# Both value projections first, the two kinds of heads in turn, the output projection in passes of six and two heads, and a square on ScalarE in the norm's Newton step

## The chip, the cores and the metric

The kernel runs on one core of one Trainium2 chip. The metric is the device time of one execution in microseconds (us). In three runs the kernel before took 1231.18, 1232.57 and 1232.76 us; the median is 1232.57 us. The engines are named as the profile names them: PE is TensorE, with PEld for its weight loads, DVE is VectorE, ACT is ScalarE, POOL is GpSimd, and SP is the queue that issues the DMAs.

## The reference

Two layers work on 512 tokens of width 1024. Each layer normalises x, projects it into seven parts of 512 columns, runs four retention heads and four stick-breaking heads of width 128, normalises each head, projects the eight heads back and adds them to x. A gated feed-forward block of width 2816 follows.

```python
h = rms_norm(x, norm1_g[l])
proj = h @ w_in[l]
rq, rk, rv, rg, sq, sk, sv = jnp.split(proj, IN_SPLITS, axis=-1)
ret = chunk_retention(apply_rotary(to_heads(rq, N_RET_HEADS)),
                      apply_rotary(to_heads(rk, N_RET_HEADS)),
                      to_heads(rv, N_RET_HEADS))
ret = from_heads(head_group_norm(ret, ret_norm_g[l])) * jax.nn.silu(rg)
sb = stick_breaking(to_heads(sq, N_SB_HEADS), to_heads(sk, N_SB_HEADS), to_heads(sv, N_SB_HEADS))
sb = from_heads(head_rms_norm(sb, sb_norm_g[l]))
x = x + jnp.concatenate([ret, sb], axis=-1) @ w_out[l]
h = rms_norm(x, norm2_g[l])
x = x + (jax.nn.silu(h @ w_gate[l]) * (h @ w_up[l])) @ w_down[l]
```

## The kernel before

Activations are held transposed: 8 tiles `x[k]` of 128 features by 512 tokens. Every fp32 matrix product is made of three fp32r matmuls on a high and a low part of both operands (`mm3`, line 184); the parts are written by ACT (`hi`) and by DVE or POOL (`lo`). Weights come as 1024-column units, each loaded by one DMA on SP and split into `whi` (ACT, line 127) and `wlo` (DVE, line 128); three units are held at a time.

The order on PE is written out by the program. The projections run one after another, and each small step of a head is put down with `pe.later(delay, fn)`, to be issued between two groups of three matmuls once the program's own count of PE time has gone by. The other engines take their work in an order that a scheduler fixes when the program is built, each strictly in turn.

In a layer the values of the stick-breaking heads come first (`SV`), then for each of four heads its `SQ`, `SK` and the gate columns `RG`, then the values of the retention heads (`RV`), then `RQ` and `RK` of four heads. A stick-breaking head makes scores (`z`), takes absolute value, exponential and logarithm on ACT (lines 513 to 515), an operation `e` and a scan on DVE (lines 516 and 523), transposes on PE (`turn`), and a product with the values (`weighted`, into bank `o`). A retention head rotates q and k (DVE lines 426 to 428, the sum on POOL in line 430), makes scores, multiplies by a decay (`p`) and makes the same product. Both end in `normed`: ACT squares the product (`sq`, line 476), the square's parts `shi` and `slo` are multiplied by ones into bank `o` (these are called the sums below), and `rsqrt` makes the inverse root from them: Ln and Exp on ACT (lines 309 and 310), then one Newton step in three DVE operations (lines 311, 314, 317), and a fourth multiplies the head by it (line 487). The head's parts `mhi` and `mlo` go into the output projection.

PSUM has three banks `acc`, four banks `z`, and a single bank `o`, which takes the product and the sums of every head in turn. The output projection takes the four stick-breaking heads for all eight tiles of x first, then the retention heads for tiles 0 to 3 and for tiles 4 to 7, in both with the last head set apart. When a tile of x is complete, `feed` makes its parts `hhi` (ACT) and `hlo` (DVE) for the feed-forward block and adds its square into `ssq` (ACT and POOL). The feed-forward block needs the sum over `ssq` (`token_scale`, parts `sshi` and `sslo`, into bank `o`) after its fourth group of weights.

Of the kernel before, what the change touches and what calls it, by code (L numbers as in the profile page):

```python
# [10 lines left out]
F32 = mybir.dt.float32  # L11
F32R = mybir.dt.float32r
# [29 lines left out]
D_RQK, D_RAV, D_SS = 9000, 9000, 5500  # L42


V_SLOT, QK_SLOT, PT_SLOT, M_SLOT = 0, 8, 12, 18


def block_plan():
# [5 lines left out]

    for l in range(L):
        plan += [("w_in", l, k, SV, 512) for k in range(KT)]
        for h in range(NH):
            for c in (SQ, SK, RG):
                plan += cols("w_in", l, c + h * HD)
        plan += [("w_in", l, k, RV, 512) for k in range(KT)]  # L60
        for h in range(NH):
            plan += cols("w_in", l, RQ + h * HD) + cols("w_in", l, RK + h * HD)
        for d in range(KT):
            plan += [("w_out", l, NH + k, d * P, P) for k in range(NH)]
        for d0 in range(0, KT, 4):
            ds = range(d0, d0 + 4)
            plan += [("w_out", l, k, d * P, P) for d in ds for k in range(NH - 1)]
            plan += [("w_out", l, NH - 1, d * P, P) for d in ds]
# [76 lines left out]
class Stream:  # L145
# [20 lines left out]
    def run(self, i):  # L166
        self.inside = True
        self.tasks.pop(i)[1]()
        self.inside = False

    def drain(self):
        while self.tasks:
            self.run(min(range(len(self.tasks)), key=lambda n: self.tasks[n][0]))

    @staticmethod
    def cost(n):
# [25 lines left out]
def layers(ctx, tc, xT_in, ws_in, gcol_in, gfin_in, cos_in, sin_in, dec_in, out):  # L202
# [137 lines left out]
    def attention(l):  # L340
        g0 = l * NG
        with tc.tile_pool(name=f"at{l}", bufs=1, reuse_waits="tile") as sb:
# [25 lines left out]
            def proj_v(col, evac):  # L368

                pss = banks_a() if col == SV else [bank() for _ in range(3)] + [bank("z", 4)]  # L370
                v = [
                    [slot(V_SLOT + TB * i + tb, n) for tb in range(TB)]
                    for i, n in enumerate(("vhi", "vlo"))
                ]

                def step(tb, k, w):
                    c = slice(tb * P, tb * P + P)
# [95 lines left out]
            def normed(o, m, key):  # L473
# [7 lines left out]
                def finish():  # L481
                    ss = bank("o", 1)
                    pe.mm(ss, ones_r, shi, True, False)
                    pe.mm(ss, ones_r, slo, False, True)
                    rn = temp("rn")
                    rsqrt(rn, ss, HD)
                    nc.vector.tensor_tensor(out=m, in0=m, in1=rn, op=ALU.mult)
                    if key < NH:
                        hi, lo = (slot(M_SLOT + 2 * key + i, n) for i, n in enumerate(("mhi", "mlo")))
                    else:  # L490
                        hi = sb.tile([P, S], F32R, tag="mhi", name="mhi", bufs=4)
                        lo = sb.tile([P, S], F32R, tag="mlo", name="mlo", bufs=4)
                    split(hi, lo, m)
                    mix[key] = hi, lo
# [95 lines left out]
            for h in range(NH):  # L590
                ps = proj(SQ + h * HD)
                q = sb.tile([P, S], F32, tag="q", name="q", bufs=1)
                nc.vector.scalar_tensor_tensor(
                    out=q, in0=ps, scalar=float(HD) ** -0.5, in1=rs, op0=ALU.mult, op1=ALU.mult
                )
                q = parts(q, "q")
                ps = proj(SK + h * HD)
                k = sb.tile([P, S], F32, tag="k", name="k", bufs=1)
                nc.vector.tensor_tensor(out=k, in0=ps, in1=rs, op=ALU.mult)
                k = parts(k, "k")  # L600
                pe.later(D_SQK, lambda h=h, q=q, k=k, v=v: stick(h, q, k, v))
                ps = proj(RG + h * HD)
                nc.vector.tensor_tensor(out=gate[:, h], in0=ps, in1=rs, op=ALU.mult)
# [8 lines left out]
            for h in range(NH):  # L612
                q = rotated(proj(RQ + h * HD), "q")
                k = rotated(proj(RK + h * HD), "k")
                pe.later(D_RQK, lambda h=h, q=q, k=k, v=v: retain(h, q, k, v))
# [5 lines left out]
            for d in range(KT):  # L621
                ps = bank()
                for k in range(NH):
                    out_step(ps, d, NH + k, k == 0, k == NH - 1)
                nc.vector.tensor_tensor(out=x[d], in0=x[d], in1=ps, op=ALU.add)
            for d0 in range(0, KT, 4):
                pss = dict(zip(range(d0, d0 + 4), banks_b() if d0 else banks_a()))
                for d, ps in pss.items():
                    for k in range(NH - 1):
                        out_step(ps, d, k, k == 0, False)  # L630
                pe.drain()
                for d, ps in pss.items():
                    out_step(ps, d, NH - 1, False, True)
                    nc.vector.tensor_tensor(out=x[d], in0=x[d], in1=ps, op=ALU.add)
                    feed(d, g0 + 8)

    def ffn(l):
        last = l == L - 1
# [176 lines left out]
```

## Time and profile before

| what | value |
|---|---|
| three runs | 1231.18, 1232.57, 1232.76 us |
| the profiled execution, its own time | 1231.52 us |
| its span, first to last instruction | 1229.7 us |
| mean granted clock of PE over the span | 0.996 |
| busy PE, PEld, DVE, ACT, POOL | 1211.7, 999.1, 693.4, 489.4, 164.9 us |
| DMA traffic over the span | 93 GB/s |

The busy time of an engine is a share of the whole span; what an engine costs the end is read from the waits and the chain. A matmul's recorded duration overlaps the next one's, so the distance from start to start, not the duration, is its price. The granted clock is given as a share: 1.00 is 2.4 GHz, 0.50 is 1.2 GHz.

### The profile page before, as it was taken

Reading aid. Unit: us, or ns where it says so; the run is one execution under the profiler, and the core shown is the slowest. Engines: PE = TensorE matmul, PEld = TensorE weight load, DVE = VectorE, ACT = ScalarE, POOL = GpSimd, SP = SyncE. Lnnn points to the kernel's source line nnn. Section 1 sums busy time; section 2 is a strip of 40 time slices with the busy share of each in tenths; the row PEclk is TensorE's granted clock in tenths of the full one; section 3 lists DMA queues with packets and bytes.
Section 4 is the critical chain, followed back from the end, with each engine's and each line's share of the span. In section 5 each row is a group of like instructions: output and inputs, shape, how many; then the busy total and the mean of one; then the engine's idle time right before and its main releaser. Section 6 shows DMA issues by size and latency. Waiting matters only on the chain.

```text
span 1229.7 us, 13902 instructions
## 1 busy us (share of the span) xinstructions
PE 1211.7 (99%) x5474; PEld 999.1 (81%) x5474; DVE 693.4 (56%) x861; ACT 489.4 (40%) x708; POOL 164.9 (13%) x142
## 2 busy tenths in 40 slices
PE   8999999999999999999999999999999999999997
PEld 6888887888888888888888888878888888888886
DVE  5557799785443344444444778997644433444433
ACT  5456643453232122233344766445433212223323
POOL 3221044030000000000112212432100000000021
PEclk9999999999999999999999999999999999999999
DMA  6221221222222322324222222212222223322221
GB/s 240 86 72 66 85 98 59 87 91 98 102 86 103 103 86 103 102 87 138 97 92 87 69 69 86 86 69 103 101 82 93 103 71 105 116 96 93 103 86 69
DMA packets 33329, 115.74 MB, mean 94 GB/s; under 512 B 3824, under 2 KB 3824, under 8 KB 33264
## 3 DMA queue, kind: packets, MB, share of 16 engines
q1 hardware_dynamic: 33120, 114.83, 27.1%
q8 instruction: 43, 0.70, 0.2%
q14 instruction: 22, 0.18, 0.0%
q10 hardware_dynamic: 144, 0.02, 0.0%
HBM read 112.75 MB, written 2.10 MB: 93 GB/s over the span
## 4 chain that ended last, share of the span: by engine, by line
PE 93%; DVE 4%; issue 2%; POOL 1%; DMA 1%; ACT 1%; SPq 0%; DVEq 0%; ACTq 0%; POOLq 0%
PE acc L181 71%; PE z L181 16%; PE o L181 4%; PE z L192 1%; DMA wraw<-ws 1%; DVE ptlo L285 1%; DVE wlo L128 1%; DVE hlo L288 0%; DVE u L311 0%; DVE mlo L285 0%; POOL slo L285 0%; DVE m L580 0%; DVE t L428 0%; DVE t L426 0%; DVE p L571 0%
## 5 line engine op out<-in xcount | busy, mean ns | idle before, releaser
L127 ACT CAST whi<-wraw 128x1024 fp32r<-128x1024 f32 (+1 forms) x205 | 214.7, 1048 | 492.2 <-PE acc L181 223.7
L181 PE MATMUL acc<-hhi,whi 128*128 128x512 f32 x960 | 376.0, 392 | 0.0
L181 PE MATMUL acc<-hhi,wlo 128*128 128x512 f32 x960 | 373.9, 389 | 0.0
L181 PE MATMUL acc<-hlo,whi 128*128 128x512 f32 x960 | 373.7, 389 | 0.0
L128 DVE TENSOR_TENSOR wlo<-wraw,whi 128x1024 fp32r<-128x1024 f32 (+1 forms) x205 | 258.0, 1259 | 131.5 <-ACT whi L127 130.7
L181 PEld LDWEIGHTS acc<-hhi,wlo 128*128 128x128 f32 x960 | 180.2, 188 | 37.9
L181 PEld LDWEIGHTS acc<-hhi,whi 128*128 128x128 f32 x960 | 180.3, 188 | 36.3
L181 PEld LDWEIGHTS acc<-hlo,whi 128*128 128x128 f32 x960 | 180.3, 188 | 36.2
L684 DVE TENSOR_TENSOR u<-acc,rs 128x512 f32<-128x512 f32 x40 | 27.7, 691 | 134.5 <-PE acc L181 134.5
L301 POOL TENSOR_TENSOR ssq<-ssq,sqx 128x512 f32<-128x512 f32 x28 | 44.7, 1598 | 392.1 <-ACT sqx L300 391.4
L681 DVE TENSOR_TENSOR g<-acc,rs 128x512 f32<-128x512 f32 x40 | 27.7, 692 | 89.9 <-PE acc L181 89.9
L181 PE MATMUL acc<-ahi,whi 128*128 128x512 f32 x176 | 68.5, 389 | 0.0
L181 PE MATMUL acc<-alo,whi 128*128 128x512 f32 x176 | 68.5, 389 | 0.0
L181 PE MATMUL acc<-ahi,wlo 128*128 128x512 f32 x176 | 68.5, 389 | 0.0
L748 POOL TENSOR_TENSOR xtd<-xtd,gfin 128x512 f32<-128x512 f32 x7 | 10.2, 1453 | 345.7 <-ACT fsq L744 345.7
L288 DVE SCALAR_TENSOR_TENSOR hlo<-x,gcol,hhi 128x512 fp32r<-128x512 f32 x32 | 38.7, 1227 | 9.0 <-ACT hhi L287 9.0
L181 PEld LDWEIGHTS acc<-alo,whi 128*128 128x128 f32 x176 | 33.0, 188 | 6.9
L181 PEld LDWEIGHTS acc<-ahi,whi 128*128 128x128 f32 x176 | 33.0, 188 | 6.8
L181 PEld LDWEIGHTS acc<-ahi,wlo 128*128 128x128 f32 x176 | 33.0, 188 | 6.8
L284 ACT CAST ahi<-u 128x512 fp32r<-128x512 f32 x44 | 27.4, 622 | 28.1 <-DVE u L685 28.1
L181 PE MATMUL z<-wlo,hhi 128*128 128x512 f32 x80 | 32.8, 410 | 2.4 <-DVE wlo L128 2.4
L181 PE MATMUL acc<-mhi,whi 128*128 128x512 f32 x88 | 35.1, 399 | 0.0
(189 smaller groups left out, 1818.1 us busy)
## 6 DMA issues: line engine op xcount, KB each, us to landing
wraw<-ws SPq DMA_DIRECT2D x203, 512.0 KB, 3.5
x<-xT SPq DMA_DIRECT2D x8, 256.0 KB, 7.1
dec<-dec SPq DMA_DIRECT2D x8, 256.0 KB, 3.7
out<-ob SPq DMA_DIRECT2D x4, 512.0 KB, 2.6
wraw<-ws SPq DMA_DIRECT2D x2, 256.0 KB, 4.1
cosrs<-cos SPq DMA_DIRECT2D x2, 256.0 KB, 5.8
sinrs<-sin SPq DMA_DIRECT2D x2, 256.0 KB, 5.4
gfin<-gfin SPq DMA_DIRECT2D x1, 512.0 KB, 4.4
```

Source lines behind the costliest of these rows:

```text
L127: nc.scalar.copy(out=hi[:, c], in_=raw[:, c])
L128: nc.vector.tensor_tensor(out=lo[:, c], in0=raw[:, c], in1=hi[:, c].bitcast(F32), op=ALU.subtract)
L181: self.nc.tensor.matmul(ps, lhsT=lhsT, rhs=rhs, start=start, stop=stop)
L192: self.nc.tensor.transpose(out, src, ident)
L284: nc.scalar.copy(out=hi, in_=src)
L285: eng.tensor_tensor(out=lo, in0=src, in1=hi.bitcast(F32), op=ALU.subtract)
L288: eng.scalar_tensor_tensor(out=lo, in0=src, scalar=scale, in1=hi.bitcast(F32), op0=ALU.mult, op1=ALU.subtract,)
L301: nc.gpsimd.tensor_tensor(out=ssq, in0=ssq, in1=q, op=ALU.add)
L681: nc.vector.tensor_tensor(out=g, in0=pg, in1=rs, op=ALU.mult)
L684: nc.vector.tensor_tensor(out=u, in0=pu, in1=rs, op=ALU.mult)
L748: nc.gpsimd.tensor_tensor(out=y, in0=y, in1=gfin[:, c], op=ALU.mult)
```

## The change

It concerns the attention part of both layers. The retention values are projected directly behind the stick-breaking values and kept in tiles of their own, since the stick-breaking values are still in use. The heads follow in the order S0 G0 S1 G1 G2 G3 R0 S2 R1 S3 R2 R3, where S is a stick-breaking head, G the gate columns of one head and R a retention head. The gate's Silu follows directly on G3. The output projection takes six heads first (the stick-breaking ones and retention heads 0 and 1): tiles 0 to 2 with four of the heads and then with the other two, tiles 3 to 7 with all six; then heads 2 and 3 for all tiles, with `feed` behind each. In the norm the square of the root is made by ACT, and three DVE operations follow instead of four. The number of matmuls and of weight units is the same.

```diff
+HEADS = [(c[0], int(c[1])) for c in "S0 G0 S1 G1 G2 G3 R0 S2 R1 S3 R2 R3".split()]
+STICKS = tuple(range(NH, 2 * NH))
+FIRST, NEXT = STICKS[:-1] + (0,), (STICKS[-1], 1)
...
+                    return sb.tile([P, S], F32R, tag=f"{n}{tb}", name=n, bufs=1)
...
-                    rn = temp("rn")
-                    rsqrt(rn, ss, HD)
-                    nc.vector.tensor_tensor(out=m, in0=m, in1=rn, op=ALU.mult)
+                    r, t = temp("rn"), temp("sq")
+                    act(out=r, in_=ss, func=AF.Ln, scale=1.0 / HD, bias=eps)
+                    act(out=r, in_=r, func=AF.Exp, scale=-0.5)
+                    act(out=t, in_=r, func=AF.Square, scale=0.125)
+                    nc.vector.scalar_tensor_tensor(
+                        out=t, in0=ss, scalar=HD * EPS, in1=t, op0=ALU.add, op1=ALU.mult
+                    )
+                    nc.vector.scalar_tensor_tensor(
+                        out=t, in0=t, scalar=6.0, in1=r, op0=ALU.subtract, op1=ALU.mult
+                    )
+                    nc.vector.scalar_tensor_tensor(
+                        out=m, in0=m, scalar=-0.25, in1=t, op0=ALU.mult, op1=ALU.mult
+                    )
...
-            v = proj_v(SV, evac_sv)
+            sv = proj_v(SV, evac_sv)
+            rv = proj_v(RV, evac_rv)
...
-            v = proj_v(RV, evac_rv)
-            pe.later(10000, silu_gate)
...
+                    if h == NH - 1:
+                        silu_gate()
...
+                while k not in mix:
+                    pe.advance()
...
+            half = FIRST + NEXT
+            pss = [bank() for _ in range(3)]
+            for d, ps in enumerate(pss):
+                for k in FIRST:
+                    out_step(ps, d, k, k == half[0], False)
+            for d, ps in enumerate(pss):
+                for k in NEXT:
+                    out_step(ps, d, k, False, k == half[-1])
+                add(d, ps)
+            for d in range(3, KT):
+                ps = bank()
+                for k in half:
+                    out_step(ps, d, k, k == half[0], k == half[-1])
+                add(d, ps)
+            pss = banks_a()
+            for d, ps in enumerate(pss):
+                out_step(ps, d, 2, True, False)
+            pe.drain()
+            for d, ps in enumerate(pss):
+                out_step(ps, d, 3, False, True)
+                add(d, ps)
+                feed(d, g0 + 8)
+            for d in range(4, KT):
+                ps = bank()
+                out_step(ps, d, 2, True, False)
+                out_step(ps, d, 3, False, True)
+                add(d, ps)
+                feed(d, g0 + 8)
```

`pe.advance()` issues the waiting step that is due first; `add` is the sum into `x[d]` on DVE.

In what follows, the PE work that lies between two instructions is counted from the order, at 0.227 us for 512 columns (1488 matmuls in 337.28 us) and in proportion for fewer.

**Place 1: a head's product in bank `o`, and what PE does next.** A name with its number is one tile. On PE before, in layer 0, the end of one retention head's product (o_1804), followed by projection (acc) and the next head's scores (z):

```order
L181 MATMUL o_1804<-ptlo_1707,vhi_1153 128x256
L181 MATMUL o_1804<-pthi_1706,vlo_1157 128x256
L181 MATMUL acc_1791<-hhi2_129,whi27_1637 128x512
L181 MATMUL acc_1791<-hlo2_137,whi27_1637 128x512
L181 MATMUL acc_1791<-hhi2_129,wlo27_1638 128x512
L181 MATMUL z_1830<-qhi_1632,khi_1729 128x512
L181 MATMUL z_1830<-qlo_1633,khi_1729 128x512
```

The next use of bank `o` before, the sums o_1877, comes behind 5.7 us of matmuls. On PE of the changed kernel, the end of the product of retention head 1 (o_1606), the sums of stick-breaking head 2 (o_1627), and projection:

```order
L186 MATMUL o_1606<-pthi_1498,vhi_387 128x256
L186 MATMUL o_1606<-ptlo_1499,vhi_387 128x256
L186 MATMUL o_1606<-pthi_1498,vlo_391 128x256
L186 MATMUL o_1627<-shi_1550,ones_r_118 128x512
L186 MATMUL o_1627<-slo_1551,ones_r_118 128x512
L186 MATMUL acc_1520<-hhi5_132,whi24_1373 128x512
```

The next use of the single bank has moved directly behind the product, with no matmul between. The operations that read o_1606 stand on DVE behind operation `e` and the scan of the next stick-breaking head (scores z_1563), then DVE's product m_1619, then ACT's square sq_1621; that square is what o_1627 waits for. From the end of z_1563 to o_1627 PE has 2.9 us of matmuls.

**Place 2: the sums of a head, and how bank `o` comes free.** On PE before, 27 matmuls (6.1 us) stand between the sums o_1877 and the next product o_1948. On ACT before, at the same sums (r_1881 is Ln, then Exp):

```order
L127 CAST whi30_1905<-wraw30_1796 128x1024
L309 ACTIVATE r_1881<-o_1877,eps_120 128x512
L310 ACTIVATE r_1881<-r_1881 128x512
L127 CAST whi31_1939<-wraw31_1909 128x1024
L284 CAST mhi_1889<-m_1817 128x512
L284 CAST khi_1900<-k_1898 128x512
L476 ACTIVATE sq_1963<-o_1948 128x512
```

On DVE lines 311 and 314 follow, the last read of the sums. On PE of the changed kernel, at the sums of stick-breaking head 3 (o_1913) and the product of retention head 2 (o_1931):

```order
L186 MATMUL o_1913<-shi_1862,ones_r_118 128x512
L186 MATMUL o_1913<-slo_1863,ones_r_118 128x512
L186 MATMUL acc_1884<-mhi_1393,whi28_1720 128x512
L186 MATMUL acc_1884<-mlo_1394,whi28_1720 128x512
L186 MATMUL acc_1884<-mhi_1393,wlo28_1721 128x512
L186 MATMUL o_1931<-pthi_1825,vhi_385 128x512
```

And on ACT there, where rn_1916 is Ln and then Exp, and sq_1917 the square that has come to ACT:

```order
L129 CAST whi30_1886<-wraw30_1791 128x1024
L289 CAST shi_1862<-sq_1860 128x512
L289 CAST khi_1879<-k_1877 128x512
L233 ACTIVATE rn_1916<-o_1913,eps_120 128x512
L129 CAST whi31_1952<-wraw31_1890 128x1024
L233 ACTIVATE rn_1916<-rn_1916 128x512
L233 ACTIVATE sq_1917<-rn_1916 128x512
L289 CAST mhi_1924<-m_1858 128x512
```

Three matmuls are left between the sums and the next product. On ACT the cast khi_1879 has moved ahead of Ln, a weight cast (whi31) between Ln and Exp, and the square behind Exp; DVE's first operation on sq_1917, the last read of o_1913, follows behind wlo31.

**Place 3: the completed tiles of x, at the end of the output projection.** On DVE before (x is the sum, hlo the low part that `feed` makes, wlo a weight unit):

```order
L634 TENSOR_TENSOR x0_86<-x0_86,z_2132 128x512
L634 TENSOR_TENSOR x1_87<-x1_87,z_2133 128x512
L634 TENSOR_TENSOR x2_88<-x2_88,z_2134 128x512
L288 SCALAR_TENSOR_TENSOR hlo0_135<-x0_86,gcol_81,hhi0_127 128x512
L634 TENSOR_TENSOR x3_89<-x3_89,z_2135 128x512
L288 SCALAR_TENSOR_TENSOR hlo1_136<-x1_87,gcol_81,hhi1_128 128x512
L128 TENSOR_TENSOR wlo36_2239<-wraw36_2186,whi36_2238 128x1024
L288 SCALAR_TENSOR_TENSOR hlo2_137<-x2_88,gcol_81,hhi2_129 128x512
L288 SCALAR_TENSOR_TENSOR hlo3_138<-x3_89,gcol_81,hhi3_130 128x512
L128 TENSOR_TENSOR wlo37_2269<-wraw37_2242,whi37_2268 128x1024
L634 TENSOR_TENSOR x4_90<-x4_90,acc_2234 128x512
L634 TENSOR_TENSOR x5_91<-x5_91,acc_2235 128x512
```

On DVE of the changed kernel, from the first completed tile on:

```order
L646 TENSOR_TENSOR x0_86<-x0_86,z_2200 128x512
L646 TENSOR_TENSOR x1_87<-x1_87,z_2201 128x512
L646 TENSOR_TENSOR x2_88<-x2_88,z_2202 128x512
L293 SCALAR_TENSOR_TENSOR hlo0_135<-x0_86,gcol_81,hhi0_127 128x512
L646 TENSOR_TENSOR x3_89<-x3_89,z_2203 128x512
L293 SCALAR_TENSOR_TENSOR hlo1_136<-x1_87,gcol_81,hhi1_128 128x512
L646 TENSOR_TENSOR x4_90<-x4_90,acc_2256 128x512
L130 TENSOR_TENSOR wlo37_2258<-wraw37_2208,whi37_2257 128x1024
L646 TENSOR_TENSOR x5_91<-x5_91,acc_2275 128x512
L293 SCALAR_TENSOR_TENSOR hlo2_137<-x2_88,gcol_81,hhi2_129 128x512
L646 TENSOR_TENSOR x6_92<-x6_92,acc_2288 128x512
L293 SCALAR_TENSOR_TENSOR hlo3_138<-x3_89,gcol_81,hhi3_130 128x512
```

The sums of tiles 4 to 7 have moved in among the low parts of tiles 0 to 3. On PE of the changed kernel 18.4 us of matmuls lie between the end of tile 0 (z_2200) and the sums of `token_scale` (o_2386); before, 23.8 us lie there.

One more move bears on a step below. In the changed kernel the last two operations of the rotation of k of retention head 2 (t2_1709) stand on DVE behind the low part of the second transposed piece of stick-breaking head 3 (z_1753) and behind another head's m_1619. From z_1753 to that retention head's scores z_1810, which need k, PE has 4.9 us of matmuls.

## Rows read from the trace of the kernel before

**Rows 1.** Page, part 1: busy us, share of the span, instructions.

```profile
PE 1211.7 (99%) x5474; PEld 999.1 (81%) x5474; DVE 693.4 (56%) x861; ACT 489.4 (40%) x708; POOL 164.9 (13%) x142
```

**Rows 2.** Chain that ended last, layer 0: start, us, what.

```profile
30.75 5.59 PE z L181 x24
...
278.39 337.28 PE acc L181 x1488
```

**Rows 3.** Waits of PE, whole span: who waited for whom: us, times, longest.

```profile
PE o L181 <- ACT shi L284: 2.6, 2, 1.3
PE z L181 <- DVE wlo L128: 2.4, 1, 2.4
PE o L181 <- POOL slo L285: 2.1, 2, 1.1
...
PE o L181 <- DVE u L314: 0.8, 2, 0.4
PE z L181 <- POOL klo L285: 0.5, 1, 0.5
```

**Rows 4.** Stretches: length, busy time (instructions) by engine, PEclk, DMA share, GB/s.

```profile
24.30:27.60 3.30, 3.30 (x9) 2.60 (x8) 1.12 (x1) 0.00 (x0) 0.00 (x0) 0.50 0.67 231
...
192.00:204.00 12.00, 9.21 (x45) 7.14 (x44) 11.63 (x16) 5.21 (x10) 5.01 (x4) 1.00 0.21 77
204.00:216.00 12.00, 11.53 (x53) 9.24 (x53) 11.91 (x15) 4.00 (x6) 4.74 (x3) 1.00 0.19 56
806.00:809.40 3.40, 3.12 (x8) 2.48 (x9) 3.40 (x4) 2.29 (x4) 1.92 (x2) 0.51 0.02 5
```

**Rows 5.** Timeline, layer 0: start, us, engine, line, operation, [idle before, releaser].

```profile
194.74 0.28 PE L181 MATMUL o<-pthi,vlo 128*128 128x256 f32 x1
...
199.69 0.74 DVE L580 SCALAR_TENSOR_TENSOR m<-o,gcol,gate 128x512 f32<-128x512 f32 x1
...
200.52 0.60 ACT L476 ACTIVATE sq<-o 128x512 f32<-128x512 f32 x1 [5.07 <-DVE m L580]
```

**Rows 6.** DVE by line and shape, 30 to 278 us: busy us, mean ns, idle.

```profile
L311 DVE SCALAR_TENSOR_TENSOR u<-r 128x512 f32<-128x512 f32 x10 | 8.4, 836 | 8.7 <-ACT r L228 6.0 <-ACT r L310 2.7
...
L314 DVE SCALAR_TENSOR_TENSOR u<-o,u 128x512 f32<-128x512 f32 x10 | 6.9, 688 | 0.2
...
L523 DVE TENSOR_TENSOR_SCAN e<-z,e 128x511 f32<-128x511 f32 x4 | 4.9, 1218 | 0.1
```

**Rows 7.** ACT by line and shape, same stretch.

```profile
L127 ACT CAST whi<-wraw 128x1024 fp32r<-128x1024 f32 x37 | 38.9, 1050 | 36.7 <-PE acc L181 20.7 <-PE z L181 8.2 <-issue 7.8
...
L309 ACT ACTIVATE r<-o,eps 128x512 f32<-128x512 f32 x8 | 5.5, 687 | 4.9 <-PE o L181 4.8
...
L310 ACT ACTIVATE r<-r 128x512 f32<-128x512 f32 x8 | 5.1, 632 | 0.2
...
L513 ACT ACTIVATE e<-z 128x512 f32<-128x512 f32 x8 | 4.6, 588 | 4.1 <-PE z L181 4.1
```

**Rows 8.** Timeline of DVE behind the first value projection, layer 0.

```profile
34.37 2.07 DVE L288 SCALAR_TENSOR_TENSOR vlo<-z,rst,vhi 128x512 fp32r<-128x512 f32 x3 [0.76 <-ACT vhi L287]
```

**Rows 9.** Page, part 6: DMA of the decay tables, KB each, us to landing.

```profile
dec<-dec SPq DMA_DIRECT2D x8, 256.0 KB, 3.7
```

**Rows 10.** POOL by line and shape, 30 to 278 us: busy us, mean ns, idle.

```profile
L301 POOL TENSOR_TENSOR ssq<-ssq,sqx 128x512 f32<-128x512 f32 x7 | 11.8, 1683 | 18.8 <-ACT sqx L300 18.6
...
L430 POOL TENSOR_TENSOR k<-t,t 128x512 f32<-128x512 f32 x4 | 7.9, 1985 | 9.3 <-DVE t L428 9.3
```

**Rows 11.** Timeline of DVE, end of the output projection of layer 0.

```profile
243.23 2.05 DVE L634 TENSOR_TENSOR x<-x,z 128x512 f32<-128x512 f32 x3 [0.82 <-PE z L181]
...
249.31 3.48 DVE L288 SCALAR_TENSOR_TENSOR hlo<-x,gcol,hhi 128x512 fp32r<-128x512 f32 x2
...
254.12 2.05 DVE L634 TENSOR_TENSOR x<-x,acc 128x512 f32<-128x512 f32 x3 [0.19 <-PE acc L181]
...
265.24 0.68 DVE L285 TENSOR_TENSOR sslo<-ssq,sshi 128x512 fp32r<-128x512 f32 x1
```

More of the change, by code (lines that the diff above doesn't have):

```diff
@@ L56, in block_plan @@
         plan += [("w_in", l, k, SV, 512) for k in range(KT)]
-        for h in range(NH):
-            for c in (SQ, SK, RG):
+        plan += [("w_in", l, k, RV, 512) for k in range(KT)]
+        for kind, h in HEADS:
+            for c in {"S": (SQ, SK), "G": (RG,), "R": (RQ, RK)}[kind]:
                 plan += cols("w_in", l, c + h * HD)
[L60 to L68, printed above, removed]
+        for ds, ks in OUT:
+            plan += [("w_out", l, k, d * P, P) for d in ds for k in ks]
         for k in range(KT):
@@ L169, in run, with advance @@
         self.inside = False
+    def advance(self):
+        self.run(min(range(len(self.tasks)), key=lambda n: self.tasks[n][0]))
     def drain(self):
         while self.tasks:
-            self.run(min(range(len(self.tasks)), key=lambda n: self.tasks[n][0]))
+            self.advance()
     @staticmethod
@@ L608, in silu_gate @@
                 table_set(EXP_LN)
-            v = proj_v(RV, evac_rv)
-            pe.later(10000, silu_gate)
[L612 to L615, printed above, removed]
+            for kind, h in HEADS:
+                if kind == "S":
+                    ps = proj(SQ + h * HD)
+                    q = sb.tile([P, S], F32, tag="q", name="q", bufs=1)
+                    nc.vector.scalar_tensor_tensor(
+                        out=q, in0=ps, scalar=float(HD) ** -0.5, in1=rs,
+                        op0=ALU.mult, op1=ALU.mult,
+                    )
+                    q = parts(q, "q")
+                    ps = proj(SK + h * HD)
+                    k = sb.tile([P, S], F32, tag="k", name="k", bufs=1)
+                    nc.vector.tensor_tensor(out=k, in0=ps, in1=rs, op=ALU.mult)
+                    k = parts(k, "k")
+                    pe.later(D_SQK, lambda h=h, q=q, k=k: stick(h, q, k, sv))
+                elif kind == "G":
+                    ps = proj(RG + h * HD)
+                    nc.vector.tensor_tensor(out=gate[:, h], in0=ps, in1=rs, op=ALU.mult)
+                    if h == NH - 1:
+                        silu_gate()
+                else:
+                    q = rotated(proj(RQ + h * HD), "q")
+                    k = rotated(proj(RK + h * HD), "k")
+                    pe.later(D_RQK, lambda h=h, q=q, k=k: retain(h, q, k, rv))
@@ L617, in out_step, with add @@
             def out_step(ps, d, k, first, last):
                 w = wst.block("w_out", l, k, d * P, P)
+                while k not in mix:
+                    pe.advance()
                 pe.mm3(ps, w, mix[k], first, last)
-            for d in range(KT):
-                ps = bank()
[L623 to L635, printed above, removed]
+            def add(d, ps):
+                nc.vector.tensor_tensor(out=x[d], in0=x[d], in1=ps, op=ALU.add)
```

24 lines of the change are left out of this document (6 added, 18 removed).

## The prediction

> **What bounds the kernel now.** I read the page's busy times first: PE is busy for 1211.7 us, 99% of the span [rows 1]. In the feed-forward part the chain of work is PE alone, 1488 matmuls in one piece of 337.28 us, 0.227 each [rows 2], and the change keeps the number of matmuls, so it can only move the time in which PE stands still or is slowed. The waits of PE come next [rows 3]: 2.6 + 2.1 + 0.8 + 0.5 = 6.0 us lie in the attention of both layers, half in each, and 2.4 us at the start, which the change doesn't touch. The table of stretches [rows 4] says why: from 192 to 216 us, where the retention heads come one upon another, DVE is busy for 23.5 of 24 us and PE stops. The timeline shows how that reaches PE [rows 5]: a head's product ended at about 195.0, DVE came to read it at 199.69, and ACT squared it at 200.52, right after DVE's reading (0.09 us behind its end); the sums wait for that square.
>
> The clock belongs to this. Behind the stop in layer 1 the granted clock is 0.51 for 3.4 us, the 1.2 GHz level [rows 4]. At half speed PE loses 1.7 us there, less the 0.3 us in which it stood still anyway (busy 3.12 of 3.40): I price such a fall at 1.4 us. The 2.4 us wait at the start was followed by one too, the equal stop in layer 0 by none. So of three stops of 2.3 to 2.4 us, two cost a fall. What the change can win is therefore 6.0 + 1.4 = 7.4 us, 0.6%.
>
> **The norm's Newton step.** Sixteen heads lose one DVE operation with two operands from SBUF (0.84 us mean [rows 6]), 13.4 us in all, and give ACT one square, priced like its Exp at 0.63 us [rows 7], 10.1 us in all. Both run beside PE; ACT is busy for some 40% of the span [rows 1], so I cost the work itself at nothing. It costs where PE waits for the end of that chain, which is in the steps below.
>
> **Both value projections first.** The second one takes the banks that the first has just filled. In the chain, PE's part of the first projection ends at 36.34 us, 30.75 + 5.59 [rows 2]. The second one's fourth bank, the only `z`, is the first one's first bank; DVE had read it out after one of three operations that began at 34.37 and took 2.07 us together [rows 8], so at about 35.1, and it is written behind nine matmuls, 2 us after 36.34. The cover is 3 us: nothing. The weight units keep their number. The gate's Silu moves to an earlier place on ACT, where no PE step is due for some us: nothing; without that cover, the ACT time of its table loads and the operation. The decay tables are still loaded by SP in front of the scores that need them, 3.7 us to landing [rows 9], behind weight loads as before: nothing, or up to 3.7 us once if one is late.
>
> **The heads in turn.** This spreads the rotations and decays of the retention heads among the stick-breaking ones, and the 6.0 us of waits should go with their cause. But the program issues small steps when its count says so, and the order of the changed kernel puts several uses of banks close together. Behind each stop all of PE's work waits, as it takes its matmuls in turn. I worked down five places of one layer by rows; both layers have the same order.
>
> (a) Scores of retention head 1 need a `z` bank from which transposed weights must be read; PE has 3.4 us, the two reads alone take 0.59 + 0.69 us [rows 6, 7], but a weight unit and a norm stand ahead of them on DVE. 0 to 1.7 us, taken 0.5.
>
> (b) Place 1: the sums directly behind a product. With empty queues the product must be read by DVE (0.74) and then by ACT (0.60) [rows 5], with hops 1.5 us: the lower end. But DVE comes to it only behind the next head's chain: Abs 0.59, Exp 0.63, the second Abs 0.59, Ln 0.63 on ACT [rows 7], then operation `e` at 0.69 and the scan at 1.22 on DVE [rows 6], then 0.74 and 0.60: 5.7 us from the end of the scores, against 2.9 us of matmuls. Taken 2.7; the upper end is the 6.1 us that the same two reads took from 195.0 to 201.1 in the trace of before [rows 5], of which I allow 4, since DVE has less queued now.
>
> The Trainium skill (PSUM — Partial Sum Buffer, PSUM bank collisions raise a hardware error) says that instructions of different engines on one bank are put one after another, two reads included. The square that began 0.09 us behind DVE's reading agrees. By reads side by side, the lower end of (b) would be about 0.9 us instead of 1.5.
>
> (c) Scores of retention head 2 wait for k, whose rotation now ends behind a transposed piece and a norm on DVE. From the end of that piece: cast 0.59, low part 0.69, `m` 0.69, two rotations 1.38, POOL's sum 1.7 to 2.0 [rows 10], cast 0.6: 5.7 to 6.0 us, with hops 6.0 to 6.4, against 4.9 us of matmuls; then POOL's low part at 1.7, less two matmuls, holds the third for about 1.1 us more. 2.2 to 2.6, taken 2.2, ends 0.5 and 3.5, as it hangs on the stop before it.
>
> (d) Place 2: a product three matmuls (0.7 us) behind the sums. Bank `o` comes free after Ln 0.69, weight cast 1.05, Exp 0.63, square 0.63 on ACT [rows 7] and one DVE operation of 0.69 [rows 6]: 3.7 us, so PE stops for 3.0 at least, and for up to 1 us more where khi holds Ln. Taken 3.3; the upper end is again the trace's 6.1 us less 0.7, about 5.
>
> (e) Place 3: in before, the low parts of the first four tiles took from 243.23 to 252.79, the last four tiles to the end of `sslo` from 254.12 to 265.92 [rows 11]: 9.6 + 11.8 = 21.4 us where the work of all eight stands in a row; PE has 18.4 us now and had 23.8. The upper end is 3.3 us with a hop. The lower is 0: seven POOL sums at 1.68 us [rows 10], 11.8, with 3.1 us of lead (a sum on DVE and four ACT operations) and 1.3 of parts fit in 18.4. Taken 1.6, the middle.
>
> Per layer 0.5 + 2.7 + 2.2 + 3.3 + 1.6 = 10.3 us, two layers 20.6 (ends 10 and 35). Of these stops (b), (c) and (d) are as long as those that cost falls of the clock: six of them, two in three, four falls, 5.6 us (ends 1 and 8 falls, 1.4 and 11.2 us).
>
> **The sum**, against the profiled execution's own 1231.52 us: 1231.5 - 7.4 + 20.6 + 5.6 = 1250.3 us. That execution stands 1 us under the median of the runs, within their spread, so I don't correct for it. I predict **1250 us**, slower by 1.5%.
>
> **The rivals.** Faster: the waits on DVE's queue go and nothing takes their place, because with DVE unburdened the reads of bank `o` keep up. It gives 1231.5 - 7.4 = 1224 us, and it holds so long as the new stops and falls sum to less than 3.7 us a layer. For it speaks that DVE is full exactly where PE stops now [rows 4] and that the norm takes 13.4 us off it; against it that (b) and (d) stop PE for 1.5 + 3.0 us even with empty queues, more than the 3.7 allowed. I give it 7%. The Trainium skill (Perfetto Trace Analysis, Optimizing Scalar/DVE Operations) says that where DVE is saturated, moving work to ScalarE may make sense; by that rule the time would be that 1224 us, and the trace bears out the saturation, but not that a longer ACT chain is free at (d).
>
> Little change: (a), (c) and (e) are covered, (b) and (d) at their lower ends, the clock falls once: 1231.5 - 7.4 + 9.0 + 1.4 = 1234.5 us, up to 1239 with one of the others. 11%.
>
> All ends at once: late steps make the next ones late, and nearly each stop costs a fall: 1231.5 - 7.4 + 35 + 11 = 1270 us; above 1262 I give 7%. That the change doesn't do what it says, with DVE as full as before so that old and new stops add, gives 1250.3 + 6.0 = 1256 us and is inside the forecast.
>
> **How the numbers follow.** The forecast, 1240 to 1262 us, has 75%; the three rivals 7, 11 and 7%. The range of 8 in 10 reaches a little into the second rival: 1238 to 1262. A measurement of this kernel can tell about 0.2%, 2.5 us, from no change. Faster by more is the first rival, 7%; within 0.2%, up to 1235 us, a third of the second, 4%; slower 89%.
>
> **What would show it.** In the waits of PE after the change: `o <- ACT sq` at 2 to 4 us, twice; `o` waiting for the first DVE operation of the norm at 3 to 5 us, twice; `z` waiting for khi and klo, 1 to 2 us each; `sslo` or `sshi` of `token_scale` up to 3 us, twice; the old waits on shi and slo at less than 1 us. In the clock, three to five stretches at 0.5 in the attention parts. The prediction is wrong if the waits of PE there are under 8 us in all, or if the clock stays at 1.0 behind stops of 3 us.

## The result and the profile after

The changed kernel took 1252.16 us (median of four runs, 1250.41 to 1253.51), the kernel before, run beside it, 1231.96 us (1231.18 to 1232.76). The ratio is 1.0164, with a 95% interval from 1.0148 to 1.018: 20 us slower. The prediction was 1250 us, with a range from 1238 to 1262. The profiled execution took 1253.51 us over a span of 1251.7 us, 22.0 us more than the span of before. Its mean granted clock is 0.989, against 0.996.

Busy time by engine, to be held against [rows 1]:

```profile
PE 1218.9 (97%) x5474; PEld 1004.1 (80%) x5474; DVE 665.6 (53%) x845; ACT 500.0 (40%) x724; POOL 160.9 (13%) x142
```

ACT gained 10.6 us for the sixteen squares, as costed (10.1). DVE lost 27.8 us, twice what was costed; 17.4 of them come with the Newton step alone, as a run below shows. PE has the same 5474 matmuls and the span is longer, so the time went into PE's standing still and into its clock. The waits of PE (who waited for whom: us, times, longest), to be held against [rows 3]:

```profile
PE o L186 <- DVE sq L497: 7.0, 2, 3.5
PE o L186 <- ACT sq L484: 4.4, 2, 2.2
PE o L186 <- DVE sslo L290: 3.6, 2, 1.8
PE z L186 <- DVE wlo L130: 3.4, 3, 2.7
PE z L186 <- POOL klo L290: 1.7, 2, 1.1
PE z L186 <- DVE ptlo L290: 1.5, 2, 0.7
PE z L186 <- ACT khi L289: 1.5, 1, 1.5
```

None of the waits of before in the attention (shi, slo, u: 5.5 us of the 6.0) is left. In their place stand 19.7 us, and each row answers to one step of the prediction: sq L497 is (d), sq L484 is (b), sslo is (e), klo and khi are (c), ptlo is (a). The wait for wlo lies at the start, as before.

The clock is the other part. Stretches of the trace (length, busy time by engine in the order PE, PEld, DVE, ACT, POOL, granted clock, DMA), behind (b) and (d) of layer 0 and behind (d) of layer 1, and two of 12 us:

```profile
180.60:183.90 3.30, 3.30 (x9) 2.61 (x10) 1.92 (x4) 2.55 (x5) 1.41 (x3) 0.55 0.00 0
192.00:204.00 12.00, 9.91 (x48) 7.53 (x47) 11.31 (x15) 5.57 (x10) 5.88 (x4) 1.00 0.26 89
204.00:216.00 12.00, 12.00 (x54) 10.22 (x53) 7.52 (x11) 4.69 (x8) 6.02 (x4) 0.86 0.02 2
221.00:224.30 3.30, 3.30 (x14) 3.06 (x13) 2.13 (x3) 0.62 (x1) 0.00 (x0) 0.52 0.36 134
832.30:835.60 3.30, 3.30 (x13) 3.10 (x12) 1.63 (x4) 0.62 (x1) 0.00 (x0) 0.51 0.40 144
```

Looked at in stretches of 1 us, the granted clock falls to 0.5, the 1.2 GHz level, for 3.4 us five times in the attention parts: behind (b), (c) and (d) in layer 0, behind (b) and (d) in layer 1. Before it fell there once. The stretch from 192 to 204 us, where DVE was busy for 11.63 us before [rows 4], still has it at 11.31, but in the next one it fell from 11.91 to 7.52, and from 168 to 228 us DVE was busy for 40.6 us in all where it was busy for 57.4 before. So the heads in turn did relieve DVE, and PE stopped all the same: (b) and (d) stand in stretches in which DVE had room.

That accounts for the span: 19.7 - 6.0 = 13.7 us of waits, and four more falls at the prediction's 1.4 us, 5.6 us: 19.3 of the 22.0. Another 1.4 us were lost at the start, which the change doesn't touch: there PE's 107th matmul, in the first value projection, began at 35.3 us instead of 33.9 in this execution. The last 1.3 us are mostly the price of the falls. By half of the time in which PE was busy at the low clock, the five cost 8.2 us and the one of before 1.5, so 6.6 us more instead of 5.6.

### The profile page after: what moved, and what is told of

Read it like the earlier page. It is cut to its first block, busy times and chain, and to the rows that moved or that the text cites. A ratio compares the mean times of both kernels' runs of the same rounds, so it can differ in the third digit from the quotient of the medians.

```text
span 1251.7 us, 13896 instructions
## 1 busy us (share of the span) xinstructions
PE 1218.9 (97%) x5474; PEld 1004.1 (80%) x5474; DVE 665.6 (53%) x845; ACT 500.0 (40%) x724; POOL 160.9 (13%) x142
## 4 chain that ended last, share of the span: by engine, by line
PE 86%; DVE 7%; ACT 2%; issue 2%; POOL 2%; DMA 1%; SPq 0%; ACTq 0%; DVEq 0%
PE acc L186 69%; PE z L186 13%; PE o L186 4%; DVE wlo L130 2%; DVE hlo L293 1%; POOL k L438 1%; DVE x L646 1%; ACT whi L129 1%; PE z L197 1%; DVE e L541 1%; DMA wraw<-ws 1%; DVE sq L497 0%; DVE e L534 0%; POOL klo L290 0%; DVE ptlo L290 0%
## 5 line engine op out<-in xcount | busy, mean ns | idle before, releaser
L186 PE MATMUL acc<-mlo,whi 128*128 128x512 f32 x112 | 44.4, 396 | 0.0
L186 PE MATMUL acc<-mhi,whi 128*128 128x512 f32 x112 | 44.3, 396 | 0.0
L186 PE MATMUL acc<-mhi,wlo 128*128 128x512 f32 x112 | 44.2, 395 | 0.0
L293 DVE SCALAR_TENSOR_TENSOR hlo<-x,gcol,hhi 128x512 fp32r<-128x512 f32 x32 | 35.2, 1117 | 9.1 <-ACT hhi L292 9.1
```

The costliest lines, as they stand in the source:

```text
L186: self.nc.tensor.matmul(ps, lhsT=lhsT, rhs=rhs, start=start, stop=stop)
L293: eng.scalar_tensor_tensor(out=lo, in0=src, scalar=scale, in1=hi.bitcast(F32), op0=ALU.mult, op1=ALU.subtract,)
```

## The experiments

**Theories.** The prediction's: the order of the heads brings uses of the one bank `o` and of `z` too close together, and each stop comes from its own chain, so it goes when that chain or bank is taken away. First rival, displacement: PE is held by how fast DVE, ACT and POOL get through their work, and a stop taken away comes back at the next place. Second rival: ACT's longer chain in the norm causes the stops. Third: each of the other parts, costed at nothing, has a price of its own.

**The order of the heads undone in the changed kernel.**

```diff
-HEADS = [... "S0 G0 S1 G1 G2 G3 R0 S2 R1 S3 R2 R3".split()]
+HEADS = [... "S0 G0 S1 G1 S2 G2 S3 G3 R0 R1 R2 R3".split()]
```

> The changed kernel, with its heads in the order of before (S0 G0 S1 G1 S2 G2 S3 G3 R0 R1 R2 R3), all else of the change kept. My theory: (a) to (d), 8.5 and 7.5 us in the two layers, and their five falls are the doing of the heads' order; they go, part of the 6.0 us of waits of before and a fall come back, (e) stays at 3.6 us: about 1237 us. The rival, that the value projection, the output passes or the norm cause them: 1248 us or more.

1240.64 us, ratio 1.0068 (1.0051 to 1.0086): 11.5 us of the 20 are gone, and the time stands 3.6 us above what the theory gave. Its waits of PE:

```profile
PE o L186 <- POOL slo L290: 3.8, 4, 1.0
PE o L186 <- DVE sslo L290: 3.6, 2, 1.8
...
PE o L186 <- DVE sq L497: 2.3, 2, 1.1
```

The stop (b) (sq L484) and those for khi, klo and ptlo are gone, and so is (d); its row (sq L497) now stands for another place, at 177 us, with 1.1 us each. sslo, (e), stays as it was. So the order of the heads makes (a) to (d), and (e) is a separate matter. The other 8 to 9 us stay without the new order. By the waits, 3.6 us of them are sslo's; slo's four waits and those at 177 us are also in the run with the value projections alone, below. No run has all three undone.

**The sums in other banks.** In the changed kernel the sums of the heads take a bank `z`, the last ones `acc`, instead of the one `o`.

```diff
-                    ss = bank("o", 1)
+                    ss = bank(*sums_in[0])
```

> The changed kernel, with the sums of a head put into a z bank (an acc bank in the last pass of the output projection) instead of the single bank o. My theory: places (b) and (d), 2.2 + 3.5 us a layer in the profile after, are waits for that one bank, so `o <- ACT sq` and `o <- DVE sq` vanish, 11.4 us, and with them the falls of the clock behind them, some four of 1.4 us: about 1235 us if nothing takes their place. The rival, that the chain of DVE, ACT and POOL is late by itself and the bank only shows it: the stops move to the next place that waits for that chain, `z` for khi at (c) from 2 to 4 or 5 us and mhi in the output projection by 1 to 2 us a layer, and the time stays at 1243 us or above.

1245.4 us, ratio 1.0109 (1.0094 to 1.0124). The waits of PE:

```profile
PE z L186 <- ACT khi L289: 8.5, 2, 4.2
PE o L186 <- DVE sslo L290: 3.6, 2, 1.8
...
PE acc L186 <- DVE mlo L290: 1.8, 2, 0.9
```

(b) and (d), 11.4 us, are gone: the single bank is their cause. But the time is 10 us above the theory's 1235, where the rival had it: (c) grew from 2.1 and 1.1 us to 4.2 in each layer, and mlo is new. Counted from the stop (a) of layer 0, PE now came to those scores after 31.4 us instead of 35.3, and khi let it go on after 35.6 instead of 36.8. Of the 3.9 us that PE came earlier, 1.2 were won and the rest became a wait: the first rival is right for that place. 11.4 us of stops taken away brought 6.8.

**token_scale later.** In the changed kernel it stands behind six groups of weights instead of four.

```diff
-                if k == 3:
+                if k == 5:
```

> The changed kernel, with the sums over ssq (token_scale of the feed-forward block) two groups of weights later. My theory: place (e), 1.8 us a layer, is a deadline that the now later feed misses; 5.4 us later it is met, so `o <- DVE sslo` vanishes and the time falls by 3.6 to 4 us, to about 1248 us. The rival, that the wait comes back where rs is needed at the end of the first group (g waits for it, its banks stay taken): no change, 1252 us.

1247.49 us, ratio 1.012 (1.0105 to 1.0135), as the theory gave. The wait for sslo, 3.6 us, is gone and 4.7 us with it; sq L497 and sq L484 stay at 7.0 and 4.4 us. Nothing came in its place: here the first rival is wrong.

**Both edits together.**

> The changed kernel with two edits together: the sums of the heads in the banks z and acc instead of o (alone 1245.4 us), and token_scale two groups later (alone 1247.5 us). Theory (the two act at separate places): the gains add, 6.8 and 4.7 us, 1240 to 1242 us, with the waits for khi (8.5 us in both layers) left and none for sslo. Rival (the sums of token_scale were late because of what the stops before had pushed back, so the same time is won twice): 1244 to 1246 us.

1241.79 us, ratio 1.0078 (1.0066 to 1.0091). Alone the edits brought 6.8 and 4.7 us, together 10.4: about their sum. The largest wait left is the one that had grown:

```profile
PE z L186 <- ACT khi L289: 8.5, 2, 4.2
```

**The Newton step of before in the changed kernel, and the new one alone in the kernel before.** In the first the lines of the norm's Newton step are undone (the part of the diff in `finish`), in the second they are the only edit.

> The changed kernel, with the norm's Newton step of before (four operations on DVE, no square on ACT). My theory: the step is no cause of the stops; bank o comes free at (d) after Ln, weight cast, Exp and two DVE operations, 3.75 us by rows 6 and 7 against 3.7, and DVE gets 13 us more work of which a part stands in the chains: 1252 us, within 3 us. The rival, that the square on ACT makes the chain at (d) long: `o <-` at (d) falls from 3.5 to under 3 us a layer and the time to 1249 us or below.

> The kernel before with only the norm's new Newton step (square on ScalarE, three DVE operations instead of four). Theory (the order of the heads causes the new stops, the Newton step is off the path or helps): where the retention heads stand in a row DVE is full, and each norm there gives back one DVE operation of 0.7 to 1.8 us, so the 6.0 us of waits before shrink by 1 to 3 us: 1229 to 1231 us. Rival (the longer chain on ScalarE makes the sums' bank come free later): the waits on bank o grow by 0.6 us at each of the 8 norms that PE waits for, up to 5 us: 1235 to 1237 us.

With the old step in the changed kernel 1254.33 us, ratio 1.0181 (1.0164 to 1.0198), which overlaps the changed kernel's interval; its longest waits are those of (d), longer than the 3.5 us with the new step:

```profile
PE o L186 <- DVE u L319: 8.4, 2, 4.3
```

The new step alone in the kernel before: 1231.32 us, ratio 0.9994 (0.9986 to 1.0003), no change. Its waits:

```profile
PE o L181 <- DVE sq L489: 2.3, 2, 1.1
PE o L181 <- POOL slo L285: 2.1, 2, 1.0
PE o L181 <- ACT shi L284: 1.3, 2, 0.6
```

The wait for shi halved from 2.6 us [rows 3] and the wait for the bank's release grew from 0.8 to 2.3: 5.7 us against 6.0. DVE was relieved by 17 us in all, and PE got 0.3. So neither the hope nor the second rival holds: the step is neutral within what these runs can tell.

**The value projections alone.** The kernel before, with only the second value projection moved in front.

```diff
-            v = proj_v(SV, evac_sv)
+            sv = proj_v(SV, evac_sv)
+            rv = proj_v(RV, evac_rv)
```

> The kernel before with only the value projection of the retention heads moved directly behind that of the stick-breaking heads, into tiles of its own. The prediction costed it at nothing: 1232 us, with the waits of PE as before (6.0 us in attention). Rival (the projection stood as a cushion of matmuls between the two kinds of heads, and without it the last stick-breaking head's steps and the first retention head's run into each other): one or two new waits of PE in each layer, 1 to 2 us a layer, with a fall of the clock up to 1238 us.

1238.01 us (1233.7 to 1238.17), ratio 1.004 (1.0024 to 1.0055): slower by 3 to 7 us, where the prediction had costed the move at nothing. The waits of PE:

```profile
PE o L181 <- POOL slo L285: 4.2, 4, 1.1
...
PE o L181 <- ACT shi L284: 2.0, 4, 0.9
```

The wait for slo comes four times instead of twice: the old pair behind a retention head at 204 us, and a new one at 188 us, right where the first retention heads now follow on the last stick-breaking one without the projection between. The clock falls twice instead of once. The third rival is right for this part.

**The output passes of before in the changed kernel.** The loops of the output projection (the last part of the diff) and the matching order of its weights are undone.

> The changed kernel with the output projection of the kernel before (four stick-breaking heads for all tiles, then the retention heads for tiles 0 to 3 and 4 to 7). Theory (the passes of six and two heads cause only the wait for sslo, 3.6 us in both layers): that wait goes, the stops in the heads remain at 16 us; retention head 3 is now wanted earlier or later by some us and may make a wait for mhi of up to 2 us a layer: 1248 to 1252 us. Rival (the passes have no part in sslo's wait): 1252 us with the wait in place.

1256.4 us, ratio 1.0203 (1.0189 to 1.0217). sslo's wait went, and the longest wait of all runs came:

```profile
PE acc L190 <- ACT mhi L293: 12.9, 2, 6.4
```

Both the theory (1248 to 1252 us) and its rival missed this. The old passes begin with the four stick-breaking heads, and the last of them is not ready: in layer 0 its sums are made at 211.7 us, and PE stands until `mhi` has come at 218.6. The row of (d) is gone here, as these are the sums of place 2: PE now stands still for the whole of that norm instead of for the bank alone. So the passes of six and two belong to the order of the heads, and in the changed kernel they cost less than what they replace.

**POOL's low parts on DVE.** The waits for slo and klo pointed to POOL. In the kernel before with the new Newton step, the low parts of q, k and of the squares (`qlo`, `klo`, `slo`) are made by DVE:

```diff
-                split(hi, lo, t, eng=nc.gpsimd)
+                split(hi, lo, t)
...
-                split(shi, slo, sq, eng=nc.gpsimd)
+                split(shi, slo, sq)
```

> The kernel before with the new Newton step and with the low parts of q, k and of the squares moved from POOL to DVE (three POOL operations of 1.4 to 1.6 us a head become three DVE operations). Theory: DVE's operations on two SBUF operands take 0.69 us alone and 1.2 to 1.8 us where POOL works beside them, so the move costs DVE less than it adds, and the waits for slo (2.1 us) and klo (0.5 us) go: 1225 to 1229 us. Rival (DVE is full where the retention heads stand in a row, and 0.7 us more a part makes the reads of the product later): the waits for shi grow by 1 to 2 us a head, 1234 to 1240 us.

1226.94 us (1225.68 to 1228.5), ratio 0.9964 (0.9951 to 0.9976): faster than both kernels. Its waits of PE in the attention are 2.7 us, and the clock does not fall there at all:

```profile
PE o L181 <- DVE slo L285: 1.3, 2, 0.7
...
PE o L181 <- ACT shi L284: 1.0, 2, 0.5
```

Busy times with the Newton step alone, and with the low parts on DVE too:

```profile
PE 1210.5 (98%) x5474; PEld 997.8 (81%) x5474; DVE 676.0 (55%) x845; ACT 498.8 (41%) x724; POOL 161.2 (13%) x142
```

```profile
PE 1209.5 (99%) x5474; PEld 997.9 (81%) x5474; DVE 693.7 (57%) x893; ACT 498.5 (41%) x724; POOL 88.5 (7%) x94
```

DVE got 48 operations more. At 0.69 us they would be 33 us; its busy time grew by 17.7. The other 15 us are what its remaining operations no longer lose to POOL: added up one by one, the durations of those 845 fell from 705.0 to 689.5 us. The timeline of this kernel shows the loss that is left (start, us, engine, line, operation):

```profile
196.78 1.28 POOL L430 TENSOR_TENSOR q<-t,t 128x512 f32<-128x512 f32 x1 [6.50 <-PE z L181]
...
197.31 1.31 DVE L285 TENSOR_TENSOR mlo<-m,mhi 128x512 fp32r<-128x512 f32 x1
...
200.13 0.67 DVE L285 TENSOR_TENSOR qlo<-q,qhi 128x512 fp32r<-128x512 f32 x1
```

Beside POOL's sum a low part takes 1.31 us and ends 0.56 us behind it, alone 0.67.

**Which half of that does it, and does more help?** The low parts alone with the old Newton step; and, on top of both edits, the rotations' sums on DVE (`nc.gpsimd.tensor_tensor(out=r, ...)` becomes `nc.vector...`).

> The kernel before with only the low parts of q, k and of the squares on DVE instead of POOL, the old Newton step left. The run with both gave 1226.9 us, the new Newton step alone 1231.3. Theory (the gain comes from POOL no longer working beside DVE, the Newton step adds little): 1227 to 1230 us, waits of PE for slo under 1.5 us in all. Rival (DVE has room for the low parts only because the new Newton step freed an operation a head): the waits for shi and u stay at 3.4 us or grow, 1231 to 1235 us.

> The kernel with both (new Newton step, low parts on DVE) with the rotations' sums of q and k on DVE too: in the attention POOL keeps only small memsets there. 16 DVE operations of 0.69 us come, 16 POOL operations of 1.6 to 2.0 us go. Theory (what POOL does beside DVE costs DVE's low parts 0.2 to 0.3 us each, seen as 0.96 and 0.89 us for qlo and mlo where alone they take 0.69): no gain left in PE's waits (2.7 us in attention), 1225 to 1228 us. Rival (DVE, full there, is now the bound): waits for shi and slo grow by 1 us or more in each layer, 1228 to 1232 us.

The low parts alone: 1229.04 us, ratio 0.9969 (0.9956 to 0.9981), so most of the gain is theirs; the waits for slo are 2.2 us, more than the 1.5 expected. With the rotations' sums too: 1228.59 us, ratio 0.9967 (0.9954 to 0.9979): no further gain, and 0.6 us above the theory's range, in the rival's. Its waits in the attention are 3.7 us instead of 2.7: shi's went and slo's halved to 0.6, but sq's grew to 1.3 and a new one came:

```profile
PE z L181 <- DVE klo L285: 1.8, 2, 0.9
```

**The same move in the changed kernel.**

> The changed kernel with the low parts of q, k and of the squares on DVE instead of POOL. Theory (the stops behind a product and behind the sums come from bank o's turn through DVE and ScalarE, not from POOL): those of 2.2 and 3.5 us stay within 0.7 us, the wait for klo (1.7 us in both layers) goes, 1248 to 1253 us. Rival (POOL beside DVE makes the long DVE queue at these places): the stops halve as they did in the kernel before, 1240 to 1246 us.

1255.65 us, ratio 1.0191 (1.0177 to 1.0204), not better than the changed kernel, above the theory's range and far above the rival's:

```profile
PE o L186 <- DVE sq L497: 5.9, 2, 2.9
PE o L186 <- ACT sq L484: 4.6, 2, 2.4
PE z L186 <- DVE klo L290: 4.0, 2, 2.8
```

(b) and (d) stay at 2.2 to 2.9 us, so POOL isn't their cause (at most 0.6 us of (d) is its doing). The wait for klo was to go and more than doubled, since the low part now queues on DVE: in layer 0 it began 1.3 us behind the end of khi, after two operations of another head's rotation.

**All runs in one account.** For each profiled execution: the waits of PE in the attention and up to token_scale (us), the number of 3.4 us stretches at half clock there (one of 6.8 counts as two), how much later than before PE's 107th matmul began (the start), what the first two columns make of the span against before (waits less 6.0, plus 1.4 a fall more than one), and the measured difference of the spans.

| kernel | waits | falls | start | worked | measured |
|---|---|---|---|---|---|
| before | 6.0 | 1 | 0 | | (1229.7) |
| before + Newton + low parts on DVE | 2.7 | 0 | -0.3 | -4.7 | -5.0 |
| the same + rotations' sums on DVE | 3.7 | 0 | 0.2 | -3.7 | -3.8 |
| before + low parts on DVE | 4.1 | 1 | 0.0 | -1.9 | -2.3 |
| before + Newton | 5.7 | 1 | -0.5 | -0.3 | -0.8 |
| before + value projections first | 8.1 | 2 | 1.1 | 3.5 | 6.5 |
| after, old order of heads | 11.6 | 2 | -0.2 | 7.0 | 8.8 |
| after, sums elsewhere, token_scale later | 12.2 | 4 | 1.2 | 10.4 | 11.9 |
| after, sums elsewhere | 15.7 | 4 | 0.3 | 13.9 | 15.0 |
| after, token_scale later | 15.9 | 5 | -0.4 | 15.5 | 15.9 |
| after | 19.7 | 5 | 1.4 | 19.3 | 22.0 |
| after, low parts on DVE | 21.2 | 5 | 0.6 | 20.8 | 24.2 |
| after, old Newton step | 21.6 | 5 | 0.3 | 21.2 | 23.0 |
| after, old output passes | 23.9 | 6 | 0.3 | 24.9 | 24.7 |

In ten of the thirteen the measured difference lies between 0.5 us under and 1.8 over the worked one; the other three are 2.7, 3.0 and 3.4 over. The start differs between kernels that are alike there, so I put it down to none of the edits. With it taken off, the rest is between -0.5 and 1.9 us, and 2.8 in the changed kernel with the low parts on DVE. With each fall priced by half of PE's busy time in it, the rest is between -0.5 and 1.7 us; that much stays without a cause.

## Why the prediction was right, point by point

**(b)**, predicted 2.7 us, came to 2.18 in both layers, by the chain that was worked down. Timeline of layer 0:

```profile
174.95 0.60 ACT L531 ACTIVATE e<-z 128x512 f32<-128x512 f32 x1 [0.52 <-PE z L186]
...
177.25 0.69 DVE L534 SCALAR_TENSOR_TENSOR e<-z,e 128x512 f32<-128x512 f32 x1 [3.65 <-ACT e L533]
...
177.98 1.22 DVE L541 TENSOR_TENSOR_SCAN e<-z,e 128x511 f32<-128x511 f32 x1
...
179.12 0.73 DVE L598 SCALAR_TENSOR_TENSOR m<-o,gcol,gate 128x512 f32<-128x512 f32 x1
...
179.88 0.60 ACT L484 ACTIVATE sq<-o 128x512 f32<-128x512 f32 x1
...
180.53 0.79 PE L186 MATMUL o<-shi,ones_r 128*128 128x512 f32 x1 [2.18 <-ACT sq L484]
```

The last matmul of the product began at 178.07; DVE, free of the scan, read it from 179.12, ACT squared it from 179.88, PE went on at 180.53. The chain took what was worked out: 5.6 us from the end of the scores' first piece (174.92, behind which ACT begins), for 5.7. The mis-sized term is PE's own work in between: 2.9 us counted by columns, 3.4 in the trace (174.92 to 178.34).

**(d)**, predicted 3.3, came to 3.5 in both layers, again by the order of ACT's queue:

```profile
216.11 0.62 ACT L289 CAST khi<-k 128x512 fp32r<-128x512 f32 x1 [3.63 <-POOL k L438]
...
216.63 0.68 ACT L233 ACTIVATE rn<-o,eps 128x512 f32<-128x512 f32 x1
...
217.22 1.03 ACT L129 CAST whi<-wraw 128x1024 fp32r<-128x1024 f32 x1
...
218.15 0.63 ACT L233 ACTIVATE rn<-rn 128x512 f32<-128x512 f32 x1
...
219.54 0.69 DVE L497 SCALAR_TENSOR_TENSOR sq<-o,sq 128x512 f32<-128x512 f32 x1
...
220.29 0.50 PE L186 MATMUL o<-pthi,vhi 128*128 128x512 f32 x1 [3.50 <-DVE sq L497]
```

khi held Ln for some tenths, as the upper end allowed, and the weight cast stands between Ln and Exp. With the old Newton step the stop was 4.1 to 4.3 us: the step that was moved to ACT shortens this chain in the changed kernel, though no sum of time shows it beyond the intervals.

**(c)**, predicted 2.2 in each layer, came to 1.5 + 0.6 = 2.1 in layer 0 and to 1.1 in layer 1: the mis-sized term in layer 1. POOL's sum explains about half of the difference. Layer 0, then layer 1:

```profile
199.14 1.23 DVE L130 TENSOR_TENSOR wlo<-wraw,whi 128x1024 fp32r<-128x1024 f32 x1
...
199.19 2.31 POOL L438 TENSOR_TENSOR k<-t,t 128x512 f32<-128x512 f32 x1 [4.16 <-DVE t L436]
...
200.28 0.68 DVE L434 TENSOR_TENSOR t<-acc,cosrs 128x512 f32<-128x512 f32 x1
...
812.56 1.30 POOL L438 TENSOR_TENSOR k<-t,t 128x512 f32<-128x512 f32 x1 [3.46 <-DVE t L436]
...
814.33 1.21 DVE L130 TENSOR_TENSOR wlo<-wraw,whi 128x1024 fp32r<-128x1024 f32 x1
...
814.59 2.08 POOL L290 TENSOR_TENSOR klo<-k,khi 128x512 fp32r<-128x512 f32 x1 [0.73 <-ACT khi L289]
```

In layer 0 DVE's wlo began 0.05 us ahead of the sum, and the sum took 2.31 us; in layer 1 wlo came behind the sum, which took 1.30, and klo was the one to take longer, 2.08. I had taken 1.7 to 2.0 for the sum from means [rows 10], in which both cases are mixed. The other half is where PE stood: it came to the scores 1.6 us behind the end of the rotation's last operation on DVE in layer 0 (199.11 to 200.74), and 2.5 us behind it in layer 1 (812.48 to 815.01).

**(a)** 0.75 for 0.5, **(e)** 1.78 for 1.6, both inside their ends; the runs bear out that (e) is the output passes' own (it stays with the old heads, goes with the old passes and with a later token_scale). The sum of the stops is 10.3 + 9.3 = 19.6 us for 20.6.

**The clock**: five falls for four. All four stops of (b) and (d) were followed by one, and of (c) the longer of the two; those of 1.8 us and less by none. The other traces don't bear this out as a rule: over all runs the same stop (b), 2.18 us long, was followed by a fall in five of nine cases, and six of seventeen stops of 1.6 to 1.9 us were (two stops within 1.5 us of each other counted as one). So "two in three" was a fair share, and that four came near five is in part luck. The price of 1.4 us was somewhat low. It takes off PE's idle time in full, which is among the waits already; half of the 3.12 us in which PE was busy is 1.56, and the five falls here cost 1.5 to 1.7 us each by the same measure.

**The sum came out closer than its terms.** The stops were 1.0 us less than worked out, the falls, less the one of before, 6.6 us instead of 4.2, and the profiled execution lost 1.4 us at the start that no term foresaw.

**What was costed at nothing** held for the norm (0.9994 alone) and failed for the value projections. That step looked at the banks that the second projection takes, and was silent on the cushion of matmuls that leaves the place between the two kinds of heads; alone in the kernel before it costs 3 to 7 us. In the changed kernel the heads are mixed and that place doesn't exist, so its share of the 20 us can't be told apart. The changed kernel with the old order of heads has the place again, and with it four waits for slo. What the changed order has of such cushions was counted place by place in (a) to (e).

**The rivals.** The faster one (1224 us) needed DVE's relief to reach PE. DVE was relieved by 27.8 us and PE stood still for 13.7 us more. The new Newton step alone moved the time by less than its interval. By the rule of the Trainium skill (Perfetto Trace Analysis, Optimizing Scalar/DVE Operations), moving work off a saturated DVE to ScalarE may make sense. Here it made neither gain nor loss (ratio 0.9994). "All ends at once" had its mechanism at work in one place (with the sums elsewhere, khi's wait doubled), but in the changed kernel the late steps did not add up beyond the middle values.

## To carry to other kernels

Where one engine is 99% busy, price a reordering by counting the matmuls between two uses of each bank and setting them against the chain of other engines' operations queued between, in their order: five such places gave 19.6 us of stops where 20.6 were worked out. Add the clock: in the changed kernel all five stops of 2.1 us or more were followed by 3.4 us at 1.2 GHz, at 1.5 to 1.7 us each, though in the other runs a stop of 2.18 us was followed by none in four of seven cases. And where work lies on POOL to spare DVE, look at what DVE does beside it: taking three low parts a head back from POOL won 3.5 us alone and 4.4 on top of the new Newton step, in the old order of heads; in the changed order it won nothing.

## What the runs showed of the hardware

In these traces a DVE operation with two operands in SBUF and a POOL operation did not run side by side. In the rows shown, whichever came second ended nearly its own length behind the other's end: in the kernel with the low parts on DVE, mlo 0.56 us behind POOL's sum (1.31 us instead of 0.67), in the changed kernel POOL's sum 2.31 us instead of 1.30 when wlo came first. DVE's operation with an operand in PSUM (`t<-acc,cosrs` at 200.28) took its usual 0.68 us in the middle of POOL's sum. Over the whole trace of before, six `mlo` beside POOL's work took 1.77 us in the median and ten without it 0.68, while `t<-acc,cosrs` took 0.69 and 0.68 us, eight times each. The Trainium skill (SBUF — State Buffer, Who interferes with whom) says that an instruction of VectorE with two SBUF inputs contends with a GpSimd instruction that reads SBUF, and that one with at most one SBUF input, outside the modes that use two ports, doesn't. The trace agrees in all three cases; what I had not expected is how much of DVE's queue it is, 15 us of 676.
